# Encoder trunk on one core: operands at multiples of 512 bytes, out-projection weights a pair ahead, taps in two early loads

## The chip, the core and the metric

The kernel runs on one core of a Trainium2 chip. Its engines work side by side and meet through semaphores: TensorE (PE: matrix products, weight loads shown as PEld), VectorE (DVE), ScalarE (ACT), GpSimd (POOL) and SyncE (SP), which here issues the loads and stores in order. The metric is device time in microseconds. Times are of one execution or the median of several; a smaller number is better.

## The reference, cut to what matters

All in fp32. Two requests share the weights: the prompt (1024 tokens, 1024 wide) and the sample (512 tokens). Layer 0 projects the normalised input to four retention heads and eight differential attention heads, gates both, and projects back. Layer 1 is a Conformer convolution module.

```python
def even_layer(x, ...):
    u = rms_norm(x, g) @ w_in_mix                    # 1024 -> 7168
    ro = head_rms(bidir_retention(...)) * silu(rg)   # 4 heads, 256 wide
    do = rms_norm(diff_attention(...)) * silu(dg)    # 8 heads, 128 wide
    return x + concatenate([ro, do]) @ w_out_mix     # 2048 -> 1024

def odd_layer(x, ...):
    a, b, gate = split(rms_norm(x, g) @ w_in_conv)   # 1024 -> 3 x 2048
    y = conv1d(a * sigmoid(b), conv_w) + conv_b      # per channel, 31 taps
    y = silu(layer_norm(y, cn_g, cn_b)) * silu(gate)
    return x + y @ w_out_conv                        # 2048 -> 1024
```

The output is rms_norm of the result, for both requests.

## The kernel before

Every product of fp32 matrices is made of three products in fp32r: each operand is split into a high part, rounded to fp32r, and the remainder, the low part; high by high, high by low and low by high are summed in PSUM (L191 to L193, L769 to L771, L1364 to L1366). A matmul has 128 rows in depth, 128 weight columns and 512 moving columns. The operand in SBUF that is streamed stands first in the names of the profile, the one that is loaded as weights second: `pp<-hw,wh`.

**Tiles.** `hw` holds the normalised input (hi and lo) of the first two token groups of 512, and between layers other things: the out-projection weights of the first half (WA), later the second half of out_conv (W2). `h2b` holds the third group in the Conformer stage, later a quarter of the out_conv weights. `wr`, `wh` and `wl`, three buffers each, are the ring of the input weights: raw, high and low (w_dma and w_split, L152 to L171). `T1` to `T5` are the head's work tiles; the out-projection uses them as slabs (the activations, hi and lo, read back from `acts`) for its first four row tiles, then tiles named `slab`. `zh` and `zl` are the split input of the last projection, five buffers each; `w2` holds a quarter of its weights. `sg` is a ring of three for the gate and small things, `yv` two buffers for the convolution's output.

**Stages in time** (from the span's start): the retention heads of the prompt and then of the sample interleaved with differential attention; to about 1450 us the last sample retention head; 1450 to 1570 the first half of the out-projection (over row tiles, WA); 1570 to 1760 its second half (WB, in tiles `wb`) with the norm of layer 1; to 2570 the Conformer projection over 16 channel tiles with the depthwise convolution on VectorE and GpSimd beside it; then layer norm and, to the end, the last projection (three token groups; per group 16 k-steps of 24 products, weights W1 and W2).

**What sets the order.** The code is written in the order wanted; weave and spread mix lists of steps by given positions between 0 and 1 (`0.4` is at two fifths of the other list). Each engine, and each queue of DMAs, then works in the order of the program, and a step waits till its tiles are free. A load is issued when the code names it, and where its buffer is not yet free, SyncE waits there, with everything behind it. Steps of load_wout (L725) at a position do everything for one pair of weight tiles: four loads into the `wr` ring (L739), a cast to high on ScalarE (L741), the low part on VectorE or GpSimd (L743).

oproj_steps (L751) loads a slab (L756) and the residual row (L758) and adds the product to it. conv_setup (L1197) brings the 31 x 2048 taps in from the HBM in four loads of 31 x 512 (L1206) through `sg`, transposes them (L1209), and makes the three tables for the convolution. It is called at 0.4 of the first channel tile. z_load and z_make (L1303, L1311) read the convolution's output and the gate back, normalise, activate, gate and split them into `zh` (ScalarE, L1321) and `zl` (GpSimd, L1322); pump keeps five ahead of the products (L1364 to L1366). The weights of the last projection come through load_wout, one pair at every second k-step of the first group.

The small tiles `rssq` and `rr` (L484, L487), `cbs`, `s1` and `s2` (L1180, L1181) have tags of their own in pools that lie ahead of the larger ones in SBUF, so their sizes set where the others start.

Of the kernel before, what the change touches and what calls it, by code (L numbers as in the profile page):

```python
# [9 lines left out]
F32 = mybir.dt.float32  # L10
# [8 lines left out]
P = 128  # L19
# [88 lines left out]
def trunk(tc, A, out_p, out_s, dbg=None):  # L108
# [255 lines left out]
    def ret_job(h, seq, rp, tabs, late=()):  # L364
# [85 lines left out]
        def fw(n):  # L450
# [23 lines left out]
            def c():  # L474
                o = op_.tile([P, 256], F32, name="o", tag="o")
                PE.matmul(o, U["sm"], R["V"][:, n, :], start=True, stop=False)
                if n > 0:
                    PE.matmul(o, R["qf"][:, n, :], U["R"], start=False, stop=(n == N - 1))
                if n < N - 1:
                    PE.matmul(o, R["qb"][:, n, :], R["L"][:, n, :], start=False, stop=True)  # L480
                U["o"] = rp.tile([P, 256], F32, name="osb", bufs=2)
                ACT.copy(U["o"], o)
                jk = rp.tile([P, 256], BF16, name="ojk", bufs=1)
                ssq = sm.tile([P, 1], F32, name="rssq")  # L484
                ACT.activation(out=jk, in_=o, func=AF.Square, accum_out=ssq)
                r = sm.tile([P, 1], F32, name="rr")
# [237 lines left out]

    def load_wout(src, k0, pool, tag, pool2=None, tag2=None):  # L725

        W = []
        steps = []

        def one(kp):  # L730
            def f():
# [3 lines left out]
                for k in range(2):  # L735
                    for c in range(2):
                        r = wpool.tile([P, 512], F32, name="wr", tag="wr", bufs=3)
                        r0 = (k0 + 2 * kp + k) * P
                        SY.dma_start(out=r, in_=src[r0:r0 + P, c * 512:(c + 1) * 512])  # L739
                        sl = slice(c * 512, (c + 1) * 512)  # L740
                        ACT.copy(h[:, k, sl], r)  # L741
                        eng = DVE if tag == "hw" and k0 == 0 else POOL
# [4 lines left out]
        for kp in range(4):  # L747
            steps.append((0.0, one(kp)))
        return W, steps

# [108 lines left out]
    tabs = {}  # L859
    WA, wa_steps = load_wout(A["w_out_mix"][0], 0, hw, "hw")  # L860
    M0, units0 = ret_job(0, 0, rpool, tabs, late=(1,))
# [146 lines left out]

    WB, wb_steps = load_wout(A["w_out_mix"][0], 8, wbp, "wb")
# [55 lines left out]
    def conv_job(t):  # L1065
# [76 lines left out]
        def join():  # L1142
            R["y"] = cp.tile([P, 2, YW], F32, name="yv", bufs=2)
            b_ = R["B"]
# [50 lines left out]
    cng = cst.tile([P, NCT], F32, name="cng")  # L1195
    cnb = cst.tile([P, NCT], F32, name="cnb")
    def conv_setup():  # L1197
        ones_sq = sgp.tile([P, P], F32, name="sg", tag="sg")
        POOL.memset(ones_sq, 1.0 / 2048)
        vraw = sgp.tile([NCT, 3, P], F32, name="sg", tag="sg")  # L1200
        for i, nm in enumerate(("conv_b", "conv_norm_g", "conv_norm_b")):
            SY.dma_start(out=vraw[:, i, :], in_=A[nm][0].rearrange("(t p) -> t p", p=P))
        wps = accp.tile([P, 512], F32, name="acc", tag="acc")
        for q in range(4):
            craw = sgp.tile([CONV_K, 512], F32, name="sg", tag="sg")
            SY.dma_start(out=craw, in_=A["conv_w"][0][:, q * 512:(q + 1) * 512])  # L1206
            for t in range(4):
                c0 = (4 * q + t) * 31
                PE.transpose(wps[:, c0:c0 + 31], craw[:, t * P:(t + 1) * P], ident[0:CONV_K, 0:CONV_K])  # L1209
        wv = wps[:, 0:NCT * CONV_K].rearrange("p (t k) -> p t k", k=CONV_K)  # L1210
# [9 lines left out]
        ACT.copy(cnb, vps[:, 2 * NCT:3 * NCT])  # L1220
        cbs = sm.tile([P, 1], F32, name="cbs")
        DVE.tensor_reduce(out=cbs, in_=cb, axis=AX.X, op=ALU.add)
# [16 lines left out]
    for t in range(NCT):  # L1239
# [10 lines left out]
    f1, f2 = s1.rearrange("p r j -> p (r j)"), s2.rearrange("p r j -> p (r j)")  # L1250
    RS, MR = f1[:, 0:NT], f2[:, 0:NT]
# [43 lines left out]
    zp = h2s.enter_context(tc.tile_pool(name="zp", bufs=2, reuse_waits="tile"))  # L1295
    W1, w1s = load_wout(A["w_out_conv"][0], 0, w2p, "w2", h2b, "h2b")
    W2, w2s = load_wout(A["w_out_conv"][0], 8, hw, "hw")
    NZ = 5
    seqk = [(g, k) for g in range(3) for k in range(16)]
# [11 lines left out]
    def z_make(m):  # L1311
# [6 lines left out]
        DVE.tensor_tensor(out=y, in0=y, in1=s, op=ALU.mult)  # L1318
        h = zp.tile([P, 512], F32R, name="zh", bufs=NZ)
        l = zp.tile([P, 512], F32R, name="zl", bufs=NZ)  # L1320
        ACT.copy(h, y)  # L1321
# [24 lines left out]
    gF = zp.tile([P, D], F32, name="gF", bufs=1)  # L1346
    wload = [None, None] + [f for _, f in w1s[2:] + w2s]

# [51 lines left out]
    for g in range(3):  # L1400
        for k in range(KT):
            if g == 0 and k % 2 == 0:
                if k // 2 + 2 < len(wload):
                    wload[k // 2 + 2]()
                if k == 8:
# [50 lines left out]
```

## Time and profile before

| | before |
|---|---|
| median of 3 runs | 2858.91 us (2856.44 to 2863.42) |
| profiled execution | 2858.97 us, its span 2857.0 us |
| mean granted TensorE clock | 0.994 |
| DVE, ACT, POOL busy | 62%, 40%, 43% |
| HBM read, written | 192.64 MB, 69.27 MB |

The page of the profile gives for each engine the busy time and for the span in 40 slices the busy share in tenths; the granted clock has a row of its own there. A wait has the engine, its line, the operation that released it, and the time; groups by line give the busy time, the mean length of one instruction and the idle time ahead of it. A matmul that takes 0.39 us in a row is followed by the next after 0.23 us, since matmuls are pipelined: the pace is read from the starts, not from the lengths.

### The profile page before, as it was taken

What the parts mean: (1) busy time and instruction counts of PE and PEld (TensorE: products, weight loads), DVE (VectorE), ACT (ScalarE), POOL (GpSimd) and SP (SyncE); (2) the same over time, 40 slices, a digit from 0 to 9 for tenths busy, and PEclk for the clock granted to TensorE, in tenths of its full rate; (3) what the DMA queues carried; (4) which work ended last, traced back from release to release, by engine and by line L of the source; (5) the groups of instructions that cost most, each with busy time, mean ns of one, the idle gap of its engine ahead of it and who ended that gap; (6) DMA issues with size and microseconds to landing.
All of it is one profiled execution on the core that took longest, in us unless ns stands there. A gap on an engine that the chain in (4) does not pass through costs nothing.

```text
span 2857.0 us, 36862 instructions
## 1 busy us (share of the span) xinstructions
PE 2801.6 (98%) x13342; PEld 2314.7 (81%) x13342; DVE 1766.5 (62%) x3112; ACT 1137.4 (40%) x2124; POOL 1218.3 (43%) x1198
## 2 busy tenths in 40 slices
PE   7999999999999999999999999999999999999998
PEld 6788888888888778888878788788888888887787
DVE  4222336777777786665241143699899999965653
ACT  4233245555555665654332033333232323334321
POOL 4244343333333435555634000466565655556331
PEclk9999999999999999999999999999999999999999
DMA  4121222111111213333366653011221121255442
GB/s 132 46 64 51 59 67 76 55 52 55 55 55 51 81 51 95 98 102 98 98 209 208 209 177 113 25 56 58 65 72 59 51 81 63 74 173 178 161 144 81
DMA packets 283574, 264.32 MB, mean 93 GB/s; under 512 B 14636, under 2 KB 231908, under 8 KB 283264
## 3 DMA queue, kind: packets, MB, share of 16 engines
q1 hardware_dynamic: 283392, 261.96, 29.3%
q8 instruction: 105, 1.72, 0.2%
q14 instruction: 77, 0.63, 0.1%
HBM read 192.64 MB, written 69.27 MB: 92 GB/s over the span
## 4 chain that ended last, share of the span: by engine, by line
PE 89%; DMA 4%; DVE 2%; issue 2%; POOL 1%; ACT 1%; SPq 0%; DVEq 0%; POOLq 0%; ACTq 0%
PE pp L193 19%; PE pp L191 19%; PE pp L192 19%; PE pp L769 2%; PE pp L771 2%; PE pp L770 2%; PE sc L616 2%; PE sc L618 2%; PE tr L656 2%; PE oc L1366 2%; PE oc L1364 2%; PE oc L1365 2%; DMA wr<-in_w_out_mix 1%; PE o L673 1%; PE o L674 1%
## 5 line engine op out<-in xcount | busy, mean ns | idle before, releaser
L191 PE MATMUL pp<-hw,wh 128*128 128x512 f32 x2112 | 866.6, 410 | 1.3 <-DVE vst L386 0.9
L193 PE MATMUL pp<-hw,wl 128*128 128x512 f32 x2112 | 829.2, 393 | 0.0
L192 PE MATMUL pp<-hw,wh 128*128 128x512 f32 x2112 | 827.5, 392 | 0.0
L169 POOL TENSOR_TENSOR wl<-wr,wh 128x512 fp32r<-128x512 f32 x320 | 460.1, 1439 | 688.3 <-ACT wh L168 666.2
L193 PEld LDWEIGHTS pp<-hw,wl 128*128 128x128 f32 x2112 | 397.0, 188 | 88.1 <-issue 0.9
L191 PEld LDWEIGHTS pp<-hw,wh 128*128 128x128 f32 x2112 | 397.8, 188 | 77.8 <-issue 1.7
L192 PEld LDWEIGHTS pp<-hw,wh 128*128 128x128 f32 x2112 | 398.4, 189 | 73.1 <-issue 0.9
L168 ACT CAST wh<-wr 128x512 fp32r<-128x512 f32 x320 | 197.2, 616 | 552.2 <-PE pp L192 433.3
L620 DVE CUSTOM_DVE_ANT_0 st<-sc,W 128x512 f32<-128x512 f32 x320 | 208.9, 686 | 64.0 <-PE sc L618 54.4
L1138 DVE SCALAR_TENSOR_TENSOR acc<-xs,wS,acc 128x777 f32<-128x777 f32 x240 | 246.1, 1025 | 1.4
L1138 DVE SCALAR_TENSOR_TENSOR acc<-X,wE,acc 128x777 f32<-128x777 f32 x240 | 246.1, 1025 | 0.6
L631 ACT ACTIVATE st<-st,nm 128x1024 f32<-128x1024 f32 (+1 forms) x192 | 192.3, 1003 | 40.9 <-DVE nm L620 20.8
L1117 POOL TENSOR_TENSOR pa<-pa,ct 128x777 f32<-128x777 f32 x96 | 179.9, 1874 | 5.9
L659 ACT CAST ah<-tr 128x512 fp32r<-128x512 f32 x160 | 93.3, 584 | 171.8 <-PE tr L656 170.5
L193 PE MATMUL pp<-h2b,wl 128*128 128x512 f32 x384 | 152.4, 397 | 0.0
L191 PE MATMUL pp<-h2b,wh 128*128 128x512 f32 x384 | 152.4, 397 | 0.0
L192 PE MATMUL pp<-h2b,wh 128*128 128x512 f32 x384 | 151.9, 396 | 0.0
L593 POOL CAST qz<-T 64x128 fp32r<-64x128 f32 x192 | 57.3, 299 | 194.5 <-PE sc L618 189.0
L1138 DVE SCALAR_TENSOR_TENSOR acc<-X,wO,acc 128x777 f32<-128x777 f32 x112 | 115.4, 1031 | 25.4 <-ACT acc L1123 22.4
L1322 POOL TENSOR_TENSOR zl<-zy,zh 128x512 fp32r<-128x512 f32 x48 | 69.8, 1465 | 111.0 <-ACT zh L1321 86.7
L660 DVE TENSOR_TENSOR al<-tr,ah 128x512 fp32r<-128x512 f32 x160 | 109.8, 687 | 11.4 <-ACT ah L659 9.9
L647 DVE SCALAR_TENSOR_TENSOR st<-st,cf 128x1024 f32<-128x1024 f32 (+1 forms) x96 | 112.8, 1176 | 2.9
(262 smaller groups left out, 5064.1 us busy)
## 6 DMA issues: line engine op xcount, KB each, us to landing
wr<-in_w_in_mix SPq DMA_DIRECT2D x224, 256.0 KB, 2.9
wr<-in_w_in_conv SPq DMA_DIRECT2D x96, 256.0 KB, 2.8
slab<-acts SPq DMA_DIRECT2D x20, 1024.0 KB, 6.7
acts<-rhl SPq DMA_DIRECT2D x48, 256.0 KB, 2.9
acts<-ahl SPq DMA_DIRECT2D x96, 128.0 KB, 2.2
sgd<-sg SPq DMA_DIRECT2D x48, 256.0 KB, 3.4
zy<-yd SPq DMA_DIRECT2D x48, 256.0 KB, 3.9
sg<-sgd SPq DMA_DIRECT2D x48, 256.0 KB, 3.1
```

The costliest lines, as they stand in the source:

```text
L168: ACT.copy(h, t)
L169: POOL.tensor_tensor(out=l, in0=t, in1=h.bitcast(F32), op=ALU.subtract)
L191: PE.matmul(ps[g], a, hh[:, k, :], start=(half == 0 and k == 0), stop=False)
L192: PE.matmul(ps[g], a, hl[:, k, :], start=False, stop=False)
L193: PE.matmul(ps[g], b, hh[:, k, :], start=False, stop=(half == 1 and k == 3))
L620: DVE.tensor_tensor_reduce(out=U["st", qq, c][:, ns], in0=sc[c], in1=R["W"][:, off:off + 512], op0=ALU.add, op1=ALU.min, scale=1.0, scalar ...
L631: ACT.activation(out=st_, in_=st_, func=AF.Exp, scale=-1.0, bias=m, accum_out=U["Z", qq][:, c:c + 1])
L647: DVE.scalar_tensor_tensor(out=a, in0=U["st", qq, 1], scalar=cf, in1=a, op0=ALU.mult, op1=ALU.add)
L659: ACT.copy(ah, tp)
L660: DVE.tensor_tensor(out=al, in0=tp, in1=ah.bitcast(F32), op=ALU.subtract)
L1117: POOL.tensor_tensor(out=R["pa"], in0=R["pa"], in1=tmp, op=ALU.add)
L1138: DVE.scalar_tensor_tensor(out=dst, in0=x, scalar=wj, in1=acc, op0=ALU.mult, op1=ALU.subtract if first and nm == "S" else ALU.add)
```

## The change

Three things are changed, and nothing in what is computed; the number of matmuls stays.

**Alignment.** The small tiles get the tags of others (`nssq`, `nr`), and `s1` and `s2` become one tile of 3200 floats. With this, every larger tile that follows starts at a multiple of 512 bytes in its partition. Before, the positions modulo 512 were: `hw` 0, `wh` and `wl` 0, `h2b` 384, `slab`, `wb` and `T1` to `T4` 384, `w2`, `zh` and `zl` 64. After, all are 0.

**Weights a pair ahead.** load_wout is cut into loads and splits, and the raw tiles come from a Stage, a list of buffers that are idle at that time: six `wst` for WA, the nine of `wr`, `wh` and `wl` for WB, the unused `zh` and `zl` and later `wh` and `wl` for W1, and `wh` and `wl` for W2. In the last projection the gate of z is loaded into `wr` in place of `sg`.

**Taps.** conv_w is loaded in two parts of 31 x 1024 into the `yv` buffers, issued ahead of the stage, and conv_setup comes at 0.55 in place of 0.4.

```diff
-                        r = wpool.tile([P, 512], F32, name="wr", tag="wr", bufs=3)
-                        r0 = (k0 + 2 * kp + k) * P
-                        SY.dma_start(out=r, in_=src[r0:r0 + P, c * 512:(c + 1) * 512])
                         sl = slice(c * 512, (c + 1) * 512)
+                        r = raw.pop((kp, k, c))
                         ACT.copy(h[:, k, sl], r)
...
+    class Stage:
+        def __init__(self, *tags):
+            self.tags, self.n = tags, -1
+        def __call__(self):
+            self.n += 1
+            pl, tg, bufs = self.tags[self.n % len(self.tags)]
+            return pl.tile([P, 512], F32, name=tg, tag=tg, bufs=bufs)
...
-            ex = seq_of([f for _, f in wa_steps[0:2]], 0.1, 0.9)
+            ex = [(0.02, wa_loads[0]), (0.3, wa_splits[0]), (0.32, wa_loads[1]), (0.6, wa_splits[1]),
+                  (0.62, wa_loads[2])]
...
-    for _, f in wa_steps[2:4]:
-        f()
+    wa_splits[2]()
+    wa_loads[3]()
+    wa_splits[3]()
...
-    weave(spread(chain_loads(itemsB)), seq_of([f for _, f in wb_steps], 0.1, 0.7))
+    weave(spread(chain_loads(itemsB)), seq_of(wb_loads, 0.02, 0.62), seq_of(wb_splits, 0.2, 0.8))
...
-    s1 = lnp.tile([P, 2, YW], F32, name="s1")
-    s2 = lnp.tile([P, 2, YW], F32, name="s2")
+    s12 = lnp.tile([P, 3200], F32, name="s12")
...
+    craw = [cp.tile([P, 2, YW], F32, name="yv", tag="yv", bufs=2).rearrange("p r j -> p (r j)")[0:CONV_K, 0:1024]
+            for _ in range(2)]
+    for q in range(2):
+        SY.dma_start(out=craw[q], in_=A["conv_w"][0][:, q * 1024:(q + 1) * 1024])
...
-        for q in range(4):
-            craw = sgp.tile([CONV_K, 512], F32, name="sg", tag="sg")
-            SY.dma_start(out=craw, in_=A["conv_w"][0][:, q * 512:(q + 1) * 512])
...
+        for t in range(NCT):
+            PE.transpose(wps[:, t * 31:t * 31 + 31], craw[t // 8][:, t % 8 * P:(t % 8 + 1) * P],
...
-        weave(spread(M), conv_steps(cur, old), [(0.4, conv_setup)] if t == 0 else [])
+        weave(spread(M), conv_steps(cur, old), [(0.55, conv_setup)] if t == 0 else [])
...
-        s = sgp.tile([P, 512], F32, name="sg", tag="sg")
+        s = wpool.tile([P, 512], F32, name="wr", tag="wr", bufs=3)
...
-    weave(spread(M[n:]), [(0.1, ln_cols), (0.3, z_first), (0.45, w1s[0][1]), (0.6, ln_rows(0)), (0.7, ln_rows(1)),
-                          (0.8, ln_rows(2)), (0.85, w1s[1][1])])
+    weave(spread(M[n:]), [(0.0, w1l[0]), (0.05, w1l[1]), (0.1, ln_cols), (0.3, z_first), (0.4, w1s[0]),
+                          (0.6, ln_rows(0)), (0.65, w1s[1]), (0.7, ln_rows(1)), (0.8, ln_rows(2))])
...
-    wload = [None, None] + [f for _, f in w1s[2:] + w2s]
+    wprep = {0: [w1l[2]], 1: [w1s[2], w1l[3]], 3: [w1s[3], w2l[0]], 5: [w2s[0], w2l[1]], 7: [w2s[1], w2l[2]],
+             9: [w2s[2], w2l[3]], 10: [w2s[3]]}
```

The order on SyncE where the second half of the out-projection is prepared (about 1540 to 1580 us; `wr<-in_w_out_mix` are weights of WB, `wr<-in_w_in_conv` those of the Conformer stage). Before:

```order
L739 DMA wr<-in_w_out_mix 128x512 x3
L758 DMA ox<-in_x_prompt 128x1024
L739 DMA wr<-in_w_out_mix 128x512 x2
L756 DMA slab<-acts 128x2x1024
L987 DMA xpart<-ox 128x1024
L739 DMA wr<-in_w_out_mix 128x512 x2
L156 DMA wr<-in_w_in_conv 128x4x128
L758 DMA ox<-in_x_prompt 128x1024
L156 DMA wr<-in_w_in_conv 128x4x128 x3
L756 DMA slab<-acts 128x2x1024
```

and after:

```order
L737 DMA wh<-in_w_out_mix 128x512
L737 DMA wl<-in_w_out_mix 128x512
L737 DMA wr<-in_w_out_mix 128x512
L772 DMA slab<-acts 128x2x1024
L1004 DMA xpart<-ox 128x1024
L156 DMA wr<-in_w_in_conv 128x4x128 x3
L774 DMA ox<-in_x_prompt 128x1024
L156 DMA wr<-in_w_in_conv 128x4x128 x3
L772 DMA slab<-acts 128x2x1024
```

The weights of WB, mixed with slabs before, are now all issued ahead of the slab shown first, through three rings in turn, and the Conformer weights follow it.

The order on TensorE around the taps (L1209 are the transposes of the taps, L1217 those of three vectors, L1224 the small sum; L191 to L193 the Conformer projection). Before:

```order
L191 MATMUL pp<-hw,wh 128x512
L1209 MATMUL acc<-cpk,sg 128x31 x4
L192 MATMUL pp<-hw,wh 128x512
L193 MATMUL pp<-hw,wl 128x512
L1209 MATMUL acc<-cpk,sg 128x31 x4
L191 MATMUL pp<-hw,wh 128x512
L192 MATMUL pp<-hw,wh 128x512
L193 MATMUL pp<-hw,wl 128x512
L1209 MATMUL acc<-cpk,sg 128x31 x4
```

and after:

```order
L193 MATMUL pp<-hw,wl 128x512
L1231 MATMUL acc<-cpk,yv 128x31 x16
L1240 MATMUL acc<-cpk,sg 128x16 x3
L191 MATMUL pp<-h2b,wh 128x512
L192 MATMUL pp<-h2b,wh 128x512
L193 MATMUL pp<-h2b,wl 128x512
L191 MATMUL pp<-h2b,wh 128x512
L1247 MATMUL acc<-nssq,sg 128x1
```

The sixteen transposes have become one block, followed by the three of the vectors, and four products later by the small sum.

The order on ScalarE ahead of the last projection (`sg<-pp` are the last two evictions of the gate, `zy` the activation of z, `zh` its cast). Before:

```order
L1095 ACTIVATE sg<-pp 128x512
L1317 ACTIVATE zy<-zy,cnb,cng 128x512
L741 CAST h2b<-wr 128x512
L1095 ACTIVATE sg<-pp 128x512
L1317 ACTIVATE zy<-zy,cnb,cng 128x512 x2
L741 CAST h2b<-wr 128x512 x2
```

and after:

```order
L1114 ACTIVATE sg<-pp 128x512
L1348 CAST zh<-zy 128x512
L749 CAST h2b<-wh 128x512
L749 CAST h2b<-wl 128x512
L1344 ACTIVATE zy<-zy,cnb,cng 128x512
L1114 ACTIVATE sg<-pp 128x512
```

Between the two evictions one cast of weights has become two, and a cast of z has come in ahead of them.

More of the change, by code (lines that the diff above doesn't have):

```diff
@@ L722, in att_job, with load_wout, load, f @@
         return M, [unit(j) for j in range(NK // 2)], load_w, first
[L725 to L730, printed above, removed]
+    def load_wout(src, k0, pool, tag, stage, pool2=None, tag2=None):
+        W, raw = [], {}
+        eng = DVE if tag == "hw" and k0 == 0 else POOL
+        def load(kp):
+            def f():
+                for k in range(2):
+                    for c in range(2):
+                        r = raw[kp, k, c] = stage()
+                        r0 = (k0 + 2 * kp + k) * P
+                        SY.dma_start(out=r, in_=src[r0:r0 + P, c * 512:(c + 1) * 512])
+            return f
+        def split(kp):
             def f():
@@ L745, in one @@
             return f
-        for kp in range(4):
-            steps.append((0.0, one(kp)))
-        return W, steps
+        return W, [load(kp) for kp in range(4)], [split(kp) for kp in range(4)]
+    class Stage:
[5 more added lines that the diff above has]
+            return pl.tile([P, 512], F32, name=tg, tag=tg, bufs=bufs)
     def oproj_steps(i, half, W, slab_alloc, x_alloc, fin):
@@ L859, in trunk @@
     tabs = {}
-    WA, wa_steps = load_wout(A["w_out_mix"][0], 0, hw, "hw")
+    WA, wa_loads, wa_splits = load_wout(A["w_out_mix"][0], 0, hw, "hw", Stage((rpool, "wst", 6)))
     M0, units0 = ret_job(0, 0, rpool, tabs, late=(1,))
@@ L1142, in join @@
         def join():
-            R["y"] = cp.tile([P, 2, YW], F32, name="yv", bufs=2)
+            R["y"] = cp.tile([P, 2, YW], F32, name="yv", tag="yv", bufs=2)
             b_ = R["B"]
@@ L1179, in trunk @@
     lnp = h2s.enter_context(tc.tile_pool(name="lnp", bufs=1, reuse_waits="tile"))
-    s1 = lnp.tile([P, 2, YW], F32, name="s1")
-    s2 = lnp.tile([P, 2, YW], F32, name="s2")
+    s12 = lnp.tile([P, 3200], F32, name="s12")
+    s1, s2 = (s12[:, i * 2 * YW:(i + 1) * 2 * YW].rearrange("p (r j) -> p r j", r=2) for i in range(2))
     sgp = h2s.enter_context(tc.tile_pool(name="sgp", bufs=3, reuse_waits="tile"))
@@ L1196, in trunk @@
     cnb = cst.tile([P, NCT], F32, name="cnb")
+    craw = [cp.tile([P, 2, YW], F32, name="yv", tag="yv", bufs=2).rearrange("p r j -> p (r j)")[0:CONV_K, 0:1024]
+            for _ in range(2)]
+    for q in range(2):
+        SY.dma_start(out=craw[q], in_=A["conv_w"][0][:, q * 1024:(q + 1) * 1024])
+    vraw = sgp.tile([NCT, 3, P], F32, name="sg", tag="sg")
+    for i, nm in enumerate(("conv_b", "conv_norm_g", "conv_norm_b")):
+        SY.dma_start(out=vraw[:, i, :], in_=A[nm][0].rearrange("(t p) -> t p", p=P))
     def conv_setup():
@@ L1199, in conv_setup @@
         POOL.memset(ones_sq, 1.0 / 2048)
-        vraw = sgp.tile([NCT, 3, P], F32, name="sg", tag="sg")
-        for i, nm in enumerate(("conv_b", "conv_norm_g", "conv_norm_b")):
-            SY.dma_start(out=vraw[:, i, :], in_=A[nm][0].rearrange("(t p) -> t p", p=P))
         wps = accp.tile([P, 512], F32, name="acc", tag="acc")
-        for q in range(4):
-            craw = sgp.tile([CONV_K, 512], F32, name="sg", tag="sg")
-            SY.dma_start(out=craw, in_=A["conv_w"][0][:, q * 512:(q + 1) * 512])
-            for t in range(4):
-                c0 = (4 * q + t) * 31
-                PE.transpose(wps[:, c0:c0 + 31], craw[:, t * P:(t + 1) * P], ident[0:CONV_K, 0:CONV_K])
+        for t in range(NCT):
+            PE.transpose(wps[:, t * 31:t * 31 + 31], craw[t // 8][:, t % 8 * P:(t % 8 + 1) * P],
+                         ident[0:CONV_K, 0:CONV_K])
         wv = wps[:, 0:NCT * CONV_K].rearrange("p (t k) -> p t k", k=CONV_K)
@@ L1220, in conv_setup @@
         ACT.copy(cnb, vps[:, 2 * NCT:3 * NCT])
-        cbs = sm.tile([P, 1], F32, name="cbs")
+        cbs = sm.tile([P, 1], F32, name="nssq")
         DVE.tensor_reduce(out=cbs, in_=cb, axis=AX.X, op=ALU.add)
@@ L1318, in z_make @@
         DVE.tensor_tensor(out=y, in0=y, in1=s, op=ALU.mult)
-        h = zp.tile([P, 512], F32R, name="zh", bufs=NZ)
-        l = zp.tile([P, 512], F32R, name="zl", bufs=NZ)
+        h = zp.tile([P, 512], F32R, name="zh", tag="zh", bufs=NZ)
+        l = zp.tile([P, 512], F32R, name="zl", tag="zl", bufs=NZ)
         ACT.copy(h, y)
@@ L1401, in trunk @@
         for k in range(KT):
-            if g == 0 and k % 2 == 0:
-                if k // 2 + 2 < len(wload):
-                    wload[k // 2 + 2]()
+            if g == 0:
+                for f in wprep.get(k, ()):
+                    f()
                 if k == 8:
```

17 lines of the change are left out of this document (10 added, 7 removed).

## The prediction

> **What bounds the kernel now.** I began with the page: the busy time per engine, and the chain of work that ended last.
>
> ```profile
> span 2857.0 us, 36862 instructions
> PE 2801.6 (98%) x13342; PEld 2314.7 (81%) x13342; DVE 1766.5 (62%) x3112; ACT 1137.4 (40%) x2124; POOL 1218.3 (43%) x1198
> PE 89%; DMA 4%; DVE 2%; issue 2%; POOL 1%; ACT 1%; SPq 0%; DVEq 0%; POOLq 0%; ACTq 0%
> ```
>
> TensorE is the bound: 98% busy, the next engine 62%. So there are two ways to win: the pauses of TensorE (2857.0 − 2801.6 = 55.4 us), or the distance from one matmul to the next. The change leaves the number of matmuls as it is. Next I read the waits of TensorE, longest first; these are the ones that the change can reach (columns: who waits, for whom; us in total, times, longest).
>
> ```profile
> PE oc L1364 <- ACT sg L1095: 5.0, 1, 5.0
> PE acc L1209 <- DMA sg<-in_conv_w: 3.7, 3, 1.7
> PE oc L1364 <- ACT zh L1321: 3.1, 1, 3.1
> PE pp L769 <- ACT hw L741: 2.2, 1, 2.2
> PE pp L769 <- DMA slab<-acts: 2.1, 1, 2.1
> PE tr L360 <- ACT vst L395: 1.3, 1, 1.3
> ```
>
> 17.4 us in six places; the remaining pauses (start, normalisations, tail) are untouched. But a pause costs more than its length. This is the timeline of TensorE behind the wait of 2.2 us (start, duration, what):
>
> ```profile
> 1480.23 0.63 PE L770 MATMUL pp<-hw,T 128*128 128x512 f32 x1
> 1483.22 0.49 PE L771 MATMUL pp<-hw,T 128*128 128x512 f32 x1
> ```
>
> Seven matmuls lie from the first to the second, 0.43 us apart, where 0.23 is usual: after the pause the clock was halved for some 3 us. Eight such intervals give 8 × 0.20 = 1.6 us on top of the 2.2.
>
> **The pace of a matmul, and the alignment.** I took the timeline again, in the Conformer projection (2300 us with no pause), where one group of tokens reads tile h2b and two groups read hw.
>
> ```profile
> 2002.92 0.40 PE L191 MATMUL pp<-h2b,wh 128*128 128x512 f32 x1
> 2004.32 0.39 PE L191 MATMUL pp<-hw,wh 128*128 128x512 f32 x1
> 2005.02 0.39 PE L191 MATMUL pp<-hw,wh 128*128 128x512 f32 x1
> 2006.38 0.39 PE L191 MATMUL pp<-hw,wh 128*128 128x512 f32 x1
> 2008.19 0.39 PE L193 MATMUL pp<-hw,wl 128*128 128x512 f32 x1
> ```
>
> With h2b, 6 matmuls take 1.40 us: 233 ns each. The first three with hw after it take 0.70: still 233. The last 8 take 1.81: 226 ns. In the built programs, h2b starts at 384 modulo 512 and its weights at 0, while hw and its weights are both at 0. So the pace goes with the difference of the two operands' positions, not with the position itself, and after a change it takes about three matmuls to settle. The output projections bear this out (hw 0 with slab 384, wb 384 with slab 384; then hw 0 with z 64, w2 64 with z 64, h2b 384 with z 64):
>
> ```profile
> 1535.22 0.40 PE L769 MATMUL pp<-hw,slab 128*128 128x512 f32 x1
> 1538.95 0.39 PE L770 MATMUL pp<-hw,slab 128*128 128x512 f32 x1
> 1651.73 0.39 PE L771 MATMUL pp<-wb,slab 128*128 128x512 f32 x1
> 1655.83 0.39 PE L771 MATMUL pp<-wb,slab 128*128 128x512 f32 x1
> 2589.74 0.39 PE L1364 MATMUL oc<-w,zh 128*128 128x512 f32 x1
> 2592.92 0.39 PE L1366 MATMUL oc<-w,zl 128*128 128x512 f32 x1
> 2659.82 0.39 PE L1364 MATMUL oc<-hw,zh 128*128 128x512 f32 x1
> 2662.85 0.39 PE L1365 MATMUL oc<-hw,zh 128*128 128x512 f32 x1
> 2799.72 0.39 PE L1366 MATMUL oc<-h2b,zl 128*128 128x512 f32 x1
> 2802.93 0.39 PE L1365 MATMUL oc<-h2b,zh 128*128 128x512 f32 x1
> ```
>
> hw with slab: 16 in 3.73, 233 ns. wb with the same slab: 18 in 4.10, 228. w2 with z: 14 in 3.18, 227; hw with z: 13 in 3.03, 233; h2b with z: 14 in 3.21, 229. Whenever the residues are equal, 226 to 228; unequal, 229 to 233. After the change all of these are 0 and 0. The terms:
> - h2b in the projection, by the grouping by line from 1800 to 2500 us (count, busy us, mean ns):
>
> ```profile
> L192 PE MATMUL pp<-hw,wh 128*128 128x512 f32 x679 | 264.6, 390 | 0.0
> L192 PE MATMUL pp<-h2b,wh 128*128 128x512 f32 x340 | 133.9, 394 | 0.0
> ```
>
>  4 ns apart in the mean, where hw holds the slow three after each switch (3 × 94 of 2304, at 6.5 ns: 0.8); the timeline gave 7. I take 5.5 for 1152 matmuls (48 weight groups, 8 deep, three products), 6.3 us, and 282 by 6.5 ns for the slow three, 1.8. Together **8.1**.
> - out-projection, hw with slab: 384 by 5.3 = **2.0**; with T, same residues, 192 by the same 5.3 = **1.0**.
> - last projection: hw with z 576 by 6.0 = **3.5**; h2b with z 288 by 2.2 = **0.6**.
> - Attention: hw and its weights are at 0 already there, but between short runs of them stand matmuls at 384. The same grouping from 1035 to 1430 us:
>
> ```profile
> L192 PE MATMUL pp<-hw,wh 128*128 128x512 f32 x399 | 156.1, 391 | 0.0
> ```
>
>  1 ns above the 390 of hw, and the attention stages hold some 2100 such matmuls (399 × 3 here and about 290 × 3 in the stretch before): 2 us. If each of them lost what h2b loses, it would be 2100 × 5 = 10. Nothing excludes 0, since the runs are short and other shapes interrupt them still. I take **3**, near the row, and keep 0 to 10.
>
> Sum of the alignment: 18.2 us.
>
> [...]
>
> **The pauses, part by part.** Taps first. Before, three of four loads of conv_w go through a ring of three buffers, and each waits for the transposes of an earlier one:
>
> ```profile
> 1785.66 0.39 PE L191 MATMUL pp<-hw,wh 128*128 128x512 f32 x1
> 1787.71 0.43 PE L1209 MATMUL acc<-cpk,sg 31*128 31x31 f32 x4 [1.66 <-DMA sg<-in_conv_w]
> 1788.06 0.50 PE L192 MATMUL pp<-hw,wh 128*128 128x512 f32 x1
> 1798.12 0.40 PE L191 MATMUL pp<-hw,wh 128*128 128x512 f32 x1
> ```
>
> From 1785.66 to 1798.12 are 12.46 us. In them lie 18 large matmuls (18 × 0.229 = 4.1) and three blocks of four transposes (0.35 each, from 1787.71 to 1788.06: 1.05). 7.3 us are lost, half of it at half clock. After: two loads into idle yv buffers, issued with the first weights of the stage, some 20 us before they are needed, so all 16 transposes run in one go. New is that the tiny matmul at L1247 stands only four matmuls (0.9 us) behind the transposes, and needs three small ScalarE copies and a VectorE sum first; queued behind it is TensorE itself. The bound is 0 to 2; I take 0.4. **−6.9**.
>
> Weights of the out-projection, WA. The 2.2 us wait for the cast of weights at 1476 us goes: three of the four pairs are loaded during the last retention head and two of them split there. The fourth pair's last two tiles are late by design (they wait for the splits of the third pair); needed at about 1475, expected at 1473. **−3.8** (2.2 + 1.6), bound 0 to 3.8. The 1.3 us at 1445 (L360) came from ScalarE stuck at a cast whose weights stood behind the eight WA loads in SyncE's queue; that cover is cleared: **−1.3**.
>
> WB. The slab at 1572 us was free, but its load stood on SyncE behind weight loads that waited for wr buffers:
>
> ```profile
> 1564.95 2.87 SPq L156 DMA_DIRECT2D wr<-in_w_in_conv  x3
> 1567.87 0.53 SPq L756 DMA_DIRECT2D slab<-acts  x1
> 1575.16 0.47 PE pp L769
> 1579.27 0.23 PE pp L770
> ```
>
> It was issued at 1567.87, 7.15 us ahead of its first use. In after seven weight loads spread over wr, wh and wl are issued, then the slab, ahead of the Conformer weights. The wait of 2.1 us goes, and with it the half clock behind it: ten matmuls from 1575.16 to 1579.27 in 4.11, at full pace 2.33, so 1.8. **−3.9**.
>
> Last projection (W1, W2). The 5.0 us wait before its first matmul is for ScalarE's eviction of the last gate group. Between the last two evictions ScalarE has an activation and a cast of h2b; after the change a cast of z and two of h2b, and the activation: two casts more, but of weights loaded earlier. I let it stay, **0**, bounds −5 to +4. The wait in the middle of the first group is another thing:
>
> ```profile
> 2646.21 0.39 PE L1366 MATMUL oc<-hw,zl 128*128 128x512 f32 x1
> 2649.67 0.50 PE L1364 MATMUL oc<-hw,zh 128*128 128x512 f32 x1 [3.07 <-ACT zh L1321]
> 2654.22 0.39 PE L1364 MATMUL oc<-hw,zh 128*128 128x512 f32 x1
> ```
>
> Ten matmuls take 8.01 us there instead of 2.33: 5.7 lost. z was late since ScalarE, which makes it, had sat at casts of W2 whose loads came through the three wr buffers. After, they come a pair ahead through wh and wl, idle by then, and z's gate through wr. **−5.7**, bounds 0 to 5.7.
>
> The extra loads go through SyncE, which is in order: behind a weight load that waits for a wh or wl buffer stand the loads of z. Work by engine is the same casts and subtractions, so nothing is added there.
>
> Pauses together: 6.9 + 3.8 + 1.3 + 3.9 + 5.7 = 21.6 us. With 18.2 the sum is 39.8. The profiled execution took 2858.97 us (span 2857.0 and 2 around it), the median of the three runs 2858.91, so 2859 − 40 = **2819 us**.
>
> [...]
>
> **Rivals.**
> - *Alignment does nothing*: the pace goes with the tile that is read, not with how two operands lie to each other. For it: I see only correlations, h2b and hw being other tiles as well. Against it: slab is the same tile in 233 and 228. Time: 2859 − 21.6 = **2837**. [...]
> - *The pauses come back as others*: the 24 products of a k-step wait for z, which waits for ScalarE or for loads. For it: in the last projection the 5.0 us wait remains, and ScalarE keeps its order. Time: 2859 − 18.2 = **2841**.
> - *All at 0 is a collision*: difference 0 at residue 0 locks only in long runs. For it: the attention rows. Then 576 with wb and 288 with w2 lose 5.5 ns each and the terms of h2b, slab and z bring nothing: +4.8 − 21.6 + 10 if attention loses as well: **2852**, no change that can be measured.
> - *Slower*: SyncE's order. In each of the 12 k-steps of the first group of the last projection, loads of W1 and W2 wait for wh or wl buffers, which POOL releases late, and z's loads stand behind them. Each late z costs what the one above cost, 5.7 us; from the seventh on (7 × 5.7 = 40) the gain is gone. All twelve: 2859 − 40 + 68 = **2887**. Against it: POOL is 43% busy, and z is loaded some steps ahead.
>
> **How the numbers follow.** Forecast 0.63, alignment nothing 0.13, pauses back 0.13, collision 0.06, slower 0.05. The range takes in the first three (0.89): down to 2819 − 7 (attention at 10) − 5 (the first wait gone) = 2807, up to 2842. A difference below 0.3% (8.6 us) can't be told from none. Faster by more: 0.63 + 0.13 + 0.13 = 0.89; within: 0.06; slower: 0.05.
>
> **What would show it.** In the timeline of after, h2b and hw with 226 to 228 ns alike, hw with slab and with z too. In the waits, the rows of the taps, of the cast of hw, of slab and of zh gone, the row of the sg eviction still near 5 us. Half-clock stretches left only at the start, the normalisations, the first matmul of the last projection and the tail. Wrong would be h2b at 232 still, or new waits for z of several us each between 2570 and 2650 us.

## The result, and the profile after

The changed kernel takes 2832.18 us (median of 4 runs, 2830.16 to 2837.2), the kernel before 2858.16: the ratio is 0.9909, 95% interval 0.989 to 0.9927, 26 us less. Forecast were 40 us less (2819), with a range of 2807 to 2842. The profiled execution took 2830.16 us.

The page of the changed kernel, span and busy time:

```profile
span 2828.4 us, 36859 instructions
PE 2777.7 (98%) x13342; PEld 2310.3 (82%) x13342; DVE 1772.2 (63%) x3112; ACT 1135.1 (40%) x2124; POOL 1213.8 (43%) x1198
```

TensorE is still the bound. Its busy time is 23.9 us less with the same 13342 matmuls, so most of the gain came from the distance between matmuls, and from half-clock stretches, which count as busy (in the kernel before, 3.42 of the 3.42 us from 1480.00 us on, at a granted clock of 0.50). Its waits (us in total, times, longest):

```profile
PE oc L1393 <- ACT sg L1114: 5.0, 1, 5.0
PE pp L785 <- DMA T<-acts: 2.8, 1, 2.8
PE oc L1393 <- ACT zh L1348: 2.7, 1, 2.7
PE pp L191 <- DVE vst L386: 1.9, 2, 1.0
```

The waits for the taps, for the cast of hw and for ScalarE's vst are gone, the slab's has shrunk to 0.3. The wait for zh, which the forecast had going, is there (3.1 before), the first slab T is waited for longer (1.3 before), and the wait for VectorE's vst (0.9 before) has a second place.

The timeline in the Conformer projection, where h2b ran at 233 ns before:

```profile
1982.46 0.39 PE L191 MATMUL pp<-h2b,wh 128*128 128x512 f32 x1
1985.18 0.39 PE L191 MATMUL pp<-hw,wh 128*128 128x512 f32 x1
1987.90 0.39 PE L191 MATMUL pp<-hw,wh 128*128 128x512 f32 x1
```

Twelve matmuls with h2b in 2.72 us, twelve with hw in 2.72: 226.7 ns each, with no slow three in between. The grouping by line of the same stage says it too (mean ns of one at the end; 390 and 394 before):

```profile
L192 PE MATMUL pp<-hw,wh 128*128 128x512 f32 x688 | 267.6, 389 | 0.0
L192 PE MATMUL pp<-h2b,wh 128*128 128x512 f32 x342 | 133.1, 389 | 0.0
```

Matmul for matmul, the start in the trace of after minus the start of the same one in the trace of before gives the time won or lost at each place (own subtraction, us, rounded; the profile of after is the fastest of its four executions, so its sum is some 3 us more than the 26 of the medians):

```
place in before                          gained    forecast
23 to 1340, retention and attention       -1.4      -3.0
1355 to 1372, new waits for vst           +2.1       0
1445, ScalarE's vst                       -1.7      -1.3
1470, first slab                          +1.3       0
1471 to 1491, cast of hw                  -4.2      -3.8
1491 to 1565 and 1585 to 1630, pace       -2.3      -3.0
1565 to 1585, slab                        -3.9      -3.9
1635, a later row                         +0.8       0
1767 to 1798, taps                        -7.9      -6.9
1800 to 2570, pace                        -8.0      -8.1
2575, first matmul of the projection       0         0
2576 to 2850, pace                        -4.4      -4.1
2646, wait for zh                         +0.5      -5.7
start of the span                         +0.3       0
sum                                      -28.9     -39.8
```

The taps, the slab and the pace came as worked out. Short of the forecast are the wait for zh (6.2 us), what the weights of WA gave back (3.4) and attention (1.6).

### The profile page after: what moved, and what is told of

It is laid out like the page before. It is cut to its first block, busy times and chain, and to the rows that moved or that the text cites. A ratio compares the mean times of both kernels' runs of the same rounds, so it can differ in the third digit from the quotient of the medians.

```text
span 2828.4 us, 36859 instructions
## 1 busy us (share of the span) xinstructions
PE 2777.7 (98%) x13342; PEld 2310.3 (82%) x13342; DVE 1772.2 (63%) x3112; ACT 1135.1 (40%) x2124; POOL 1213.8 (43%) x1198
## 5 line engine op out<-in xcount | busy, mean ns | idle before, releaser
L191 PE MATMUL pp<-hw,wh 128*128 128x512 f32 x2112 | 866.2, 410 | 2.4 <-DVE vst L386 1.9
L193 PE MATMUL pp<-hw,wl 128*128 128x512 f32 x2112 | 826.8, 391 | 0.0
L193 PEld LDWEIGHTS pp<-hw,wl 128*128 128x128 f32 x2112 | 396.8, 188 | 87.8 <-issue 0.9
L191 PEld LDWEIGHTS pp<-hw,wh 128*128 128x128 f32 x2112 | 397.5, 188 | 77.9 <-issue 1.7
L191 PE MATMUL pp<-h2b,wh 128*128 128x512 f32 x384 | 149.6, 390 | 0.0
L193 PE MATMUL pp<-h2b,wl 128*128 128x512 f32 x384 | 149.4, 389 | 0.0
L237 POOL TENSOR_SCALAR nr<-nssq 128x1 f32<-128x1 f32 x35 | 9.1, 260 | 253.0 <-ACT slab L1046 188.1
```

The lines of the kernel that those rows point to most:

```text
L191: PE.matmul(ps[g], a, hh[:, k, :], start=(half == 0 and k == 0), stop=False)
L193: PE.matmul(ps[g], b, hh[:, k, :], start=False, stop=(half == 1 and k == 3))
```

## Experiments

**Matmuls alone, by position.** A kernel of its own, with tiles m and w at given positions; the products are those of L191 to L193. The core of it:

```diff
+            for k in range(n):
+                PE.matmul(o, W[b][0], M[a][0], start=(k == 0), stop=False)
+                PE.matmul(o, W[b][0], M[a][1], start=False, stop=False)
+                PE.matmul(o, W[b][1], M[a][0], start=False, stop=(k == n - 1))
```

> Matmuls alone: the same three fp32r products as in the kernel (128x512 moving, 128x128 weights), 16 times in a row, for each pair of a moving tile at 0, 64, 128, 256, 384 modulo 512 and a weight tile at 0, 16, 32, 64, 128, 256, 384, 512 (another multiple) and 640; nothing else of the kernel is computed. No other engine or transfer works meanwhile. Theory (relative position of the two operands): equal residues 226 to 228 ns from start to start, at whatever common position, 512 as good as 0; unequal 229 to 234 ns. Rival 1 (tile or place, not relation): all pairs alike, within 1 ns. Rival 2 (collision with other engines' traffic, which is missing here): all pairs at 226 or less. Rival 3 (only position 0 is good): the pairs 64/64, 128/128, 256/256, 384/384 at 232 like the unequal ones.

The mean distance of starts in ns, from the trace, the first ten of each block left out:

```
weights at   moving at 0     64     128    256    384
0                226.7   228.9   232.3  226.7  233.3
64               233.3   226.8   228.9  233.3  228.8
128              232.2   233.3   226.8  233.3  226.7
256              226.7   228.9   232.3  226.7  233.3
384              233.3   233.3   226.7  233.3  226.7
512              226.7   228.9   232.3  226.7  233.3
640              233.3   233.3   226.7  233.3  226.7
16               233.3   231.8   226.7  233.3  226.7
32               233.3   233.4   233.4  233.3  233.2
```

Theory in its main point: the same tile m0 runs at 226.7 or at 233.3 by where the weights lie, with no other engine at work, so it is neither the tile nor other traffic, and any common position of those tried will do (226.7 or 226.8). But its period is 256 bytes, not 512: 0 with 256 and 128 with 384 are as good as equal (226.7). The table gives the four paces of the kernel before, too, by moving minus weights modulo 256: h2b with the projection's weights and hw with slab lie at 128 (233 in the kernel, 233.3 here), hw with z at 192 (233 and 233.3), h2b with z at 64 (229 and 228.8), wb with slab and w2 with z at 0 (227 to 228 and 226.7 to 226.8). The odd 226.7 with weights at 16, of moving 128 and of moving 384 (both at distance 112), was taken up again in the last of these runs.

The entries differ by up to 6.7 ns, 3%, with the distance of the two positions, so the pace hangs on both operands together. What makes it so is not shown: the runs show the pace alone.

**The alignment alone, on the kernel before.**

```diff
-                ssq = sm.tile([P, 1], F32, name="rssq")
+                ssq = sm.tile([P, 1], F32, name="nssq")
...
-                r = sm.tile([P, 1], F32, name="rr")
+                r = sm.tile([P, 1], F32, name="nr")
...
-        cbs = sm.tile([P, 1], F32, name="cbs")
+        cbs = sm.tile([P, 1], F32, name="nssq")
...
-    s1 = lnp.tile([P, 2, YW], F32, name="s1")
-    s2 = lnp.tile([P, 2, YW], F32, name="s2")
+    s12 = lnp.tile([P, 3200], F32, name="s12")
```

> The kernel before with the alignment edits alone (all operands at 0 modulo 512), weights and taps loaded as before. Theory: the pace terms of the prediction, 8 us in the Conformer projection, 3 in the first half of the out-projection, 4 in the last projection, 0 to 3 in attention: 15 to 18 us less, about 2842; the waits of 3.7, 2.2, 2.1 and 1.3 us stay. Rival (alignment does nothing, the pace belongs to the tiles): 2858, h2b still at 233 ns.

2847.23 us, ratio 0.9953 (0.9937 to 0.997): 13 us less than the 2860.17 of the kernel before on the same chip. The subtraction of starts gives the pace in full: 7.9 in the Conformer projection, 3.6 in the last one, 2.5 in the out-projection, 1.5 in attention, 15.5 together. Part of it is given back where slabs are loaded; its waits there:

```profile
PE pp L769 <- DMA slab<-acts: 4.3, 3, 3.1
PE tr L255 <- DVE ox L246: 3.2, 2, 2.1
```

2.1 and 0.7 us before. TensorE, faster there, met slabs and rows that came no earlier. The profile, 9.8 us shorter than that of the kernel before, also holds 1.4 us more at the start of the span.

**The order of z on ScalarE.** The wait for zh in the trace of the changed kernel, seen from ScalarE (zy the activation of z, zh its cast):

```profile
2608.81 0.82 ACT L1344 ACTIVATE zy<-zy,cnb,cng 128x512 f32<-128x512 f32 x1 [5.47 <-DVE zy L1343]
2611.78 0.81 ACT L1344 ACTIVATE zy<-zy,cnb,cng 128x512 f32<-128x512 f32 x1 [2.15 <-DVE zy L1343]
2612.50 1.13 ACT L1348 CAST zh<-zy 128x512 fp32r<-128x512 f32 x2
2619.14 0.82 ACT L1344 ACTIVATE zy<-zy,cnb,cng 128x512 f32<-128x512 f32 x1 [5.51 <-DVE zy L1343]
2622.10 0.81 ACT L1344 ACTIVATE zy<-zy,cnb,cng 128x512 f32<-128x512 f32 x1 [2.15 <-DVE zy L1343]
2622.82 1.12 ACT L1348 CAST zh<-zy 128x512 fp32r<-128x512 f32 x2
```

Two activations, then two casts, of the two z before. And the chain of waits between them:

```profile
2613.24 1.29 POOL zl L1349
2614.55 1.23 DMA zy<-yd
```

The cast lets GpSimd make zl, that frees one of the four zy buffers, into which the next z is loaded, whose activation stands ahead of the next cast. It is a ring of 10.3 us for two z; TensorE is never asked in it. No weight of W2 stands in it either. So the edit puts the activation of z number m behind the cast of number m−2:

```diff
-        ACT.activation(out=y, in_=y, func=AF.Silu, scale=cng[:, k:k + 1], bias=cnb[:, k:k + 1])
+        with (tc.issue_after(zcast[m - 2]) if m >= 2 else ExitStack()):
+            ACT.activation(out=y, in_=y, func=AF.Silu, scale=cng[:, k:k + 1], bias=cnb[:, k:k + 1])
...
-        ACT.copy(h, y)
+        zcast[m] = ACT.copy(h, y).ins
```

> The changed kernel, with one edit: on ScalarE the activation of z number m stands behind the cast of z number m-2. Theory (ScalarE's order holds z back: two activations, whose loads wait for the buffers that the casts release, stand ahead of two casts): the wait for zh near 2620 us (2.7 us and the half clock behind it) goes, 4 to 6 us less than the changed kernel. Rival (weights of W2 on their way through SyncE or POOL hold z back): the wait stays within 1 us of 2.7.

The wait for zh is gone, and ScalarE now waits for TensorE to free a zh, as it should where z is ahead:

```profile
2612.61 0.82 ACT L1345 ACTIVATE zy<-zy,cnb,cng 128x512 f32<-128x512 f32 x1 [2.08 <-DVE zy L1343]
2613.33 0.60 ACT L1349 CAST zh<-zy 128x512 fp32r<-128x512 f32 x1
2614.66 0.82 ACT L1345 ACTIVATE zy<-zy,cnb,cng 128x512 f32<-128x512 f32 x1 [0.73 <-DVE zy L1343]
2618.49 0.62 ACT L1349 CAST zh<-zy 128x512 fp32r<-128x512 f32 x1 [3.01 <-PE oc L1395]
```

At that place 6.2 us are won against the changed kernel. The time of this one execution, 2829.62 us, shows it hardly: 1.6 us more went at its start, 1.7 at 1471 us to a half clock that the other profile had been spared, 1.0 at 2552 to a longer one, 0.6 at a slab, and the rest in smaller pieces. The total was settled by the fourth run below.

**PSUM waits tile by tile.** The first matmul of the last projection waits 5.0 us for the last gate eviction (ScalarE, L1114). It writes a bank that had long been free; the bank of that eviction is written by the sixteenth matmul. The pool is what waits, as a whole:

```diff
-    oc = ps2.enter_context(tc.tile_pool(name="oc", bufs=8, space=PSUM))
+    oc = ps2.enter_context(tc.tile_pool(name="oc", bufs=8, space=PSUM, reuse_waits="tile"))
```

> The changed kernel, with one edit: the PSUM pool of the last projection waits tile by tile and not for the whole pool before. The first matmul then waits for an early bank only, and the sixteenth for the last gate eviction. Theory (the 5.0 us wait is one for the whole pool, but z is the next bound, since its times on ScalarE don't move): the first wait falls from 5.0 to under 2 us, and the wait for zh further on grows by about as much, so that the total is within 2 us of the changed kernel. Rival (z has slack): 4 to 6.5 us less.

```profile
PE oc L1393 <- ACT zh L1348: 5.9, 2, 4.1
PE oc L1393 <- ACT sg L1114: 1.6, 1, 1.6
```

As the theory has it: 5.0 has become 1.6, 2.7 has become 5.9, and the time is 2831.12 us. By the subtraction of starts 5.0 us are won at the first matmul and 5.8 lost at the waits for zh. A wait that another one stands behind gives nothing when it is taken away alone.

**Both edits, and the changed kernel beside it.**

> The changed kernel with both edits, the order of z on ScalarE and the PSUM waits by tile. Theory (each of the two waits is covered by the other cause when it is taken away alone): the first wait of 5.0 us falls to about 1.6, the one for zh stays away, 6 to 10 us less than the changed kernel, 2820 to 2826 us. Rival (z's own loads and buffers bind next): a wait for zh of 2 us or more remains, under 4 us gained.

> The changed kernel once more, in as many rounds on the same chip, to set e4 against: within 0.3% of 2832 us.

With both, 2821.61 us (2819.49 to 2823.34), ratio to the kernel before 0.9871 (0.9855 to 0.9888); the changed kernel on the same chip 2832.54 (2829.82 to 2837.36), 0.9913 (0.9898 to 0.9927). That is 11 us, and the intervals lie apart. By the subtraction of starts, against the profile shown above, 5.0 us are won at the first matmul of the last projection and 6.2 at the place of zh. So the expectation was wrong in one point: only the first wait was covered by the other, since the order of z won its 6.2 at the place alone as well. No wait for zh is left among its waits; of the last projection only this remains:

```profile
PE oc L1394 <- ACT sg L1114: 1.6, 1, 1.6
```

It is the fastest version measured, ahead of both kernels.

**The weights W1 and W2 as before, in the changed kernel.** load_wout of the kernel before is put back for these two, with its positions, and z's gate goes through sg again.

```diff
-    W1, w1l, w1s = load_wout(A["w_out_conv"][0], 0, w2p, "w2", stage1, h2b, "h2b")
-    W2, w2l, w2s = load_wout(A["w_out_conv"][0], 8, hw, "hw", w_bufs)
+    W1, w1s = load_wout_b(A["w_out_conv"][0], 0, w2p, "w2", h2b, "h2b")
+    W2, w2s = load_wout_b(A["w_out_conv"][0], 8, hw, "hw")
```

> The changed kernel with the loading of W1, W2 and of z's gate as before (through wr, and sg). Theory (z is held by ScalarE's order, not by weights on the way): the first wait 5.0 and the wait for zh 2 to 4 us as with the change, within 2 us of the changed kernel. Rival (the new way of loading did take something off, and the wait that is left is a rest): 4 us or more longer, the wait for zh 4 us or more.

2831.38 us in one execution, the first wait 5.0 us, the one for zh 1.8: as the changed kernel. The new way of loading W1 and W2 won nothing that can be measured.

**The z order alone, on the kernel before.** The edit is that of the second experiment.

> The kernel before with the order of z on ScalarE alone (the activation of z number m behind the cast of number m-2). Theory (that order was what made z late in the kernel before, too, where the prediction blamed the weights of W2): the waits for zh (3.1 us) and zl (0.7) go there. Rival (the weights of W2 hold ScalarE through the ring of three): the wait for zh stays at 2 us or more.

2856.12 us in one execution, which lies within the spread of the kernel before. The waits for zh and zl are gone from the list; at 2646 us 5.7 us are won by the subtraction of starts, 2.9 are lost ahead of it, 2.0 of them at a slab and 0.8 at the start. So that order, not the weights of W2, was the cause in the kernel before, too. The profile of the kernel before, without the edit, has ScalarE in the pattern of the second experiment:

```profile
2623.03 0.62 ACT L741 CAST hw<-wr 128x512 fp32r<-128x512 f32 x1 [1.44 <-DMA wr<-in_w_out_conv]
2628.92 1.24 ACT L741 CAST hw<-wr 128x512 fp32r<-128x512 f32 x2 [0.33 <-DMA wr<-in_w_out_conv]
...
2638.11 0.82 ACT L1317 ACTIVATE zy<-zy,cnb,cng 128x512 f32<-128x512 f32 x1 [2.15 <-DVE zy L1316]
2638.84 1.12 ACT L1321 CAST zh<-zy 128x512 fp32r<-128x512 f32 x2
2645.34 0.82 ACT L1317 ACTIVATE zy<-zy,cnb,cng 128x512 f32<-128x512 f32 x1 [5.38 <-DVE zy L1316]
2648.30 0.81 ACT L1317 ACTIVATE zy<-zy,cnb,cng 128x512 f32<-128x512 f32 x1 [2.15 <-DVE zy L1316]
2649.02 1.12 ACT L1321 CAST zh<-zy 128x512 fp32r<-128x512 f32 x2
```

ScalarE did wait for weights of W2, as the prediction read, but the last time at 2629 us, and for 0.33. From 2630 us to TensorE's wait at 2647 it has activations and casts of z alone, 10.2 us for two z.

**The weights WA as before, in the changed kernel.**

```diff
-            ex = [(0.02, wa_loads[0]), (0.3, wa_splits[0]), (0.32, wa_loads[1]), (0.6, wa_splits[1]),
-                  (0.62, wa_loads[2])]
+            ex = seq_of([f for _, f in wa_steps[0:2]], 0.1, 0.9)
...
-    wa_splits[2]()
-    wa_loads[3]()
-    wa_splits[3]()
+    for _, f in wa_steps[2:4]:
+        f()
```

> The changed kernel with the loading of WA as before (eight tiles during the last retention head through wr, eight at its end). Theory (the early loads took away 3.8 and 1.3 us and gave back 2 us in waits for VectorE, which makes WA's low parts, and 1 to 1.5 in the first slab): the cast of hw is waited for again (2 us and half clock) and the vst of ScalarE too, the two waits for the vst of VectorE are gone, 1.5 to 3 us longer than the changed kernel. Rival (the part is worth its whole term): 5 us longer.

2826.68 us. By the subtraction of starts that is 2.8 less than the changed kernel's profile, of which 3.3 lie at the start of the span, before WA is touched; the rest is 0.5 more. Its waits:

```profile
PE pp L811 <- DMA T<-acts: 1.9, 1, 1.9
PE tr L360 <- ACT vst L395: 1.2, 2, 1.0
PE pp L191 <- DVE vst L386: 1.0, 1, 1.0
```

The waits for VectorE's vst fell (2.1 us by the subtraction at 1355 to 1364) and ScalarE's vst came back (2.1 at 1444 to 1447), as expected. What did not come back is the cast of hw: 0.2 us where it was 2.2. The last tiles of WA were cast 4.9 us after the issue of their loads there, against 6.4 in the kernel before; why isn't settled. The wait was 2.2, 2.2 and 2.8 us in the three kernels that load both WA and WB as before (the kernel before, the alignment alone, and the z order alone on the kernel before), and 0.2 and none in the two with WA as before and WB new; so the new loads of WB, three of which stand ahead of the last loads of WA here, may be what took it off, which is not shown. What the early loads of WA are worth is about nothing. To be sure, both edits and WA as before together:

> The changed kernel with both edits of the fourth run and the loading of WA as before. Theory (WA's early loads give back what they take): within 3 us of the fourth run, 2818 to 2824 us. Rival (they are worth 5 us): 2826 or more.

2822.31 us (2821.92 to 2823.61), ratio 0.9873 (0.9853 to 0.9892): the same as the fourth run.

**Taps and WB as before, in the changed kernel.** Both are the code of the kernel before.

```diff
-    WB, wb_loads, wb_splits = load_wout(A["w_out_mix"][0], 8, wbp, "wb", idle)
+    WB, wb_steps = load_wout_b(A["w_out_mix"][0], 8, wbp, "wb")
...
-        weave(spread(M), conv_steps(cur, old), [(0.55, conv_setup)] if t == 0 else [])
+        weave(spread(M), conv_steps(cur, old), [(0.4, conv_setup)] if t == 0 else [])
```

> The changed kernel with the taps and the weights WB loaded as before; the two act at places far apart, at about 1570 and 1780 us, and are told apart by the trace. Theory (the terms of the prediction, which the trace of the changed kernel bears out): the waits for conv_w come back with 3 to 4 us and a half clock, 6 to 8 us at that place; a wait for a slab of about 2 us and a half clock comes back near 1565 us, 2 to 4 us; together 8 to 12 us longer than the changed kernel. Rival (the stage of the slabs is bound by its transfers, so that a wait saved there comes back at the next slab): 6 to 8 us in all, and nothing from WB.

2841.52 us, ratio 0.9935 (0.9918 to 0.9951), 9 us above the changed kernel's medians, as the theory has it.

```profile
PE acc L1255 <- DMA sg<-in_conv_w: 4.2, 3, 2.5
PE pp L811 <- DMA slab<-acts: 2.8, 2, 1.9
```

By the subtraction of starts, 9.3 us come back at the taps, where the half clock lasted 10.2 us against 6.8 in the kernel before, and 4.4 near 1560 us. The two are more than the 9 us of the medians, since 1.0 us was won near 1470 and 1.6 at the wait for zh, and since the profile set against it is the fastest of the changed kernel.

**Positions again, and pauses.** The matmuls alone with finer positions, forward and backward, then pauses:

```diff
+        for rep in range(10):
+            for j in (1, 2, 3, 4, 5, 6):
+                for _ in range(j):
+                    ACT.mul(g[:, 0:512], o, 0.002)
```

> Matmuls alone again, nothing else of the kernel is computed: moving tiles at 0, 64 and 128, weight tiles at every multiple of 16 from 0 to 256, 48 matmuls each, forward and then in the opposite order; then 60 pauses of about 1 to 4 us (TensorE waits for 1 to 6 copies of ScalarE), each followed by 30 to 42 matmuls. Theory for the first half (only the distance modulo 256 counts): 226 to 228 ns at distance 0 and 256, 229 to 234 at all others, alike in both directions; the odd value of the first run at 112 (226.7) is either a second such distance, then seen again here in both directions, or left over from the block ahead of it. For the second half: if the half clock goes by the length of the pause alone, there is one length that parts pauses with it from those without; if by windows that run on their own, the same length of 2 to 3 us shows both.

The timeline of three blocks, m0 with w0, with w128 and with w256, from the 21st matmul to the 48th:

```profile
35.98 0.39 PE L66 MATMUL o<-m,w 128*128 128x512 f32 x1
42.10 0.39 PE L66 MATMUL o<-m,w 128*128 128x512 f32 x1
...
302.66 0.40 PE L66 MATMUL o<-m,w 128*128 128x512 f32 x1
308.96 0.39 PE L66 MATMUL o<-m,w 128*128 128x512 f32 x1
...
570.08 0.39 PE L66 MATMUL o<-m,w 128*128 128x512 f32 x1
576.20 0.39 PE L66 MATMUL o<-m,w 128*128 128x512 f32 x1
```

27 distances in 6.12, 6.30 and 6.12 us: 226.7, 233.3 and 226.7 ns. Of all positions tried, the distance moving minus weights gives, modulo 256, in both directions: 0: 226.7; 16: 226.7 (228.3 at moving 128); 64: 228.8 to 229.0; all others between 229.8 and 234.3, but for one. That one is 112 at moving 128: 226.7 forward, 233.4 backward, and 233.3 to 233.4 at moving 0 and 64; so there the distance is not what counts alone. Whether it comes from the blocks ahead of it, which differ, is not shown.

## Why the prediction was right in its direction and too large in size

- **Alignment, 18.2 us forecast.** Right: 15.5 alone, some 16 with the rest. The terms of the Conformer projection (8.1, measured 8.0) and of the last one (4.1, measured 4.4) stood on rows of the same shape. Attention was put at 3 and gave 1.4 to 1.5; that its runs of matmuls are short, and the pace settles only after some (in the Conformer projection before, the first three with hw behind h2b still took 233 ns each), is an estimate of the reason and was not measured there. The explanation by residues of 512 was too narrow: with matmuls alone, 0 with 256 and 128 with 384 took 226.7 ns like equal positions, so it is the distance modulo 256 that went with the pace, but for the values at 112.
- **Taps, 6.9.** Right: 7.9 at the place, 9.3 when undone. The half clock there lasted 6.8 us in the kernel before and 10.2 when undone.
- **WB and the slab, 3.9.** Right: 3.9 there, 4.4 when undone. A part came back later in the stage (0.8 at 1635 us), which the forecast had at nothing. (The 7.15 us read there are the time of the slab's load; its first use came 7.29 us after the issue, and nothing hangs on it.)
- **WA, 3.8 and 1.3.** The rows of these two waits were read rightly and they are gone, but the step left out what the splits do where they were moved to: VectorE makes WA's low parts and evacuates the retention head (vst), so TensorE waited for it, 2.1 us; and the first slab came 1.3 us later in the schedule. With WA as before, the total is the same, and the cast is hardly waited for (0.2 us), so no early load of WA was needed for the larger term; what took that wait off stays open.
- **W1 and W2, 5.7: the step that failed.** It said that z was late "since ScalarE, which makes it, had sat at casts of W2 whose loads came through the three wr buffers". In the runs z is late with W2 loaded in either way (2.7 and 1.8 us), and not late with either when a cast stands ahead of the next activations. ScalarE waited at activations of z whose buffers it had not freed, which its rows showed in the profile of before as well as now. The order of ScalarE was known to be unchanged in that stretch, and the prediction itself names it in its second rival; it should have been counted as evidence against the term.
- **First matmul of the last projection, 0.** Right in the result, in part by luck, for a cause that wasn't seen: a whole pool waits, for a bank that is not the first one to be written.
- **Half clock behind the pauses.** The terms with it held at the taps and the slab. But at this length of pause it comes or not (behind 6 of 10 pauses of 2.17 us below) by how the pause falls in time, so each such term is uncertain by the 1.6 to 1.8 us that stood in it.

Of the rivals, that pauses come back as others was true of WA (3.4 us of new waits for the 5.1 that went), and its mechanism, z that waits for a ScalarE with its order kept, is what held in the last projection; that the alignment does nothing, or that common positions collide, fell with the matmuls alone.

## What to carry to other kernels

Where TensorE is the bound, compare the distance of starts between groups of the same shape: 3% lay in where two operands start to each other (226.7 against 233.3 ns), and by the matmuls alone common multiples of 256 bytes would have done (0 with 256: 226.7). Before a wait is put down to a transfer, follow the ring of buffers behind the row that releases it: here an engine's own order held its buffers, and one of two waits gave nothing until the other was gone. Work that is moved ahead into idle buffers takes its casts and subtractions along; here they went to a stretch where TensorE waits for VectorE, 2.1 us more of it.

## What the runs showed of the hardware that was not expected

The pace of TensorE hung on how its two operands lay to each other. With matmuls alone, it was 226.7 or 226.8 ns where the moving operand lies 0 bytes beyond the weights modulo 256, 226.7 or 228.3 at 16, 228.8 to 229.0 at 64, and 229.8 to 234.3 at all other distances but for the odd 226.7 at 112.

A pause of 2 us had half clock behind it in some cases and not in others. Two of the pauses made for it, both of 2.01 us, as the timeline has them:

```profile
1258.36 0.77 PE L86 MATMUL o<-m,gap 128*128 128x512 f32 x1 [2.01 <-ACT gap L82]
1258.93 0.63 PE L87 MATMUL o<-m,w 128*128 128x512 f32 x1
1259.36 0.63 PE L88 MATMUL o<-m,w 128*128 128x512 f32 x1
...
1327.22 0.50 PE L86 MATMUL o<-m,gap 128*128 128x512 f32 x1 [2.01 <-ACT gap L82]
1327.56 0.39 PE L87 MATMUL o<-m,w 128*128 128x512 f32 x1
1327.79 0.40 PE L88 MATMUL o<-m,w 128*128 128x512 f32 x1
```

After the first the matmuls are 0.43 us apart, after the second 0.23. Counted over the 60 pauses, by the gap of starts less one matmul:

```
pause us     half clock near it
0.85 to 1.54      0 of 20
2.17              6 of 10
2.80              7 of 10
3.43              8 of 10
4.06 to 4.35     10 of 10
```

Behind the pauses of 2.17 and 2.80 us the half clock lasted 3.4 us wherever it came. So it is not the length of the pause alone that decides.

The records of the granted clock in the traces say more (own counting, pauses measured as in the table). The 32 stretches of half clock in this run start whole multiples of 3.413 us apart, wherever the pauses lie. In the kernel before they do so too: after the one at 1480.00 us, those at 1575.58, 1790.62, 2575.68 and 2650.78 us come 28, 91, 321 and 343 times 3.413 us later. With the time of the run with the pauses cut at its multiples into windows of 3.413 us, none of the 41 at full clock that hold 0.7 to 1.9 us of pause had half clock behind it, and all 25 with more than 2.1 us had it; between the two lie 8, of which 6 had it. In the twelve profiles of whole kernels, from 30 to 2800 us, it is 0 of 108 and 40 of 40, with 3 of 6 between. Three windows of the run with the pauses that were themselves at half clock had another behind them with less, 1.0 to 1.2 us of pause.

So in these runs a pause of 2.2 us had half clock behind it where nearly all of it fell into one window, and none where a boundary cut it. This is some of the spread from run to run: the pause for the first slab, 2.80 us in the changed kernel, lies 1.4 us on each side of a boundary and had no half clock behind it; in the run with the order of z alone 2.7 of its 3.0 us fall into one window, and 3.4 us of half clock follow.
